# Row normalisation by the sum of absolute values: one tensor_scalar per row in place of one broadcast tensor_tensor per tile

## Chip, cores, metric

One core of one Trainium2 chip. The metric is the device time of one execution in microseconds. Every kernel is timed in the same rounds as the kernel before, on the same chip; a run counts as slow when it lies over 1.5% above the fastest of the same kernel. "Landing" of a transfer is the moment when all of its data has arrived.

## The reference

```python
x = randn(32, 512, 1024).astype(float32)
sums = np.sum(np.abs(x), axis=-1, keepdims=True)
out = (x / (sums + 1e-8)).astype(np.float32)
```

16384 rows of 1024 fp32 values: 67.1 MB are read and 67.1 MB written, 134.2 MB in all.

## The kernel before

Each of the 128 partitions gets 128 rows, cut into ten tiles of 12 rows and a last one of 8. A tile is 48 KB in each partition (6.29 MB in all), and there are four buffers. SyncE issues loads, ScalarE issues stores. A load can go only when the store that last used its buffer has landed: the fifth load is issued at 73.36 us, and the first store lands at 73.4.

```python
R = 12; BUFS = 4; HEAD = 32
rows = [R] * ((per_partition - HEAD) // R + 2) + [HEAD - 2 * R]   # 12 x10, 8
sbuf  = tile_pool(bufs=BUFS); stats = tile_pool(bufs=4)

def normalize(x_tile, r0, k, kv):
    nc.vector.tensor_reduce(out=s[:, :k], in_=x_tile[:, r0:r0+k, :], axis=X,
                            op=add, apply_absolute_value=True)
    nc.vector.tensor_scalar_add(out=s[:, :k], in0=s[:, :k], scalar1=EPS)
    nc.vector.reciprocal(out=inv[:, :k], in_=s[:, :k])
    nc.vector.tensor_mul(                       # rows 0..kv: one broadcast multiply
        out=x_tile[:, r0:r0+kv, :], in0=x_tile[:, r0:r0+kv, :],
        in1=inv[:, :kv].unsqueeze(2).to_broadcast([P, kv, d]))
    for r in range(kv, k):                      # rows kv..k: ScalarE
        nc.scalar.activation(out=row, in_=row, func=Copy, scale=inv[:, r:r+1])

for i, k in enumerate(rows):
    x_tile = sbuf.tile([P, R, d], FP32)
    nc.sync.dma_start(out=x_tile[:, :k, :], in_=piece(x_flat, i))
    if i == 0: normalize(x_tile, 0, k, k - 5)   # five rows of the first tile to ScalarE
    else:      normalize(x_tile, 0, k, k - 1 if i + BUFS < len(rows) else k)
    nc.scalar.dma_start(out=piece(out_flat, i), in_=x_tile[:, :k, :])
# ... launch and the definition of piece() cut
```

## Time and profile before

| what | value |
|---|---|
| time, median (lowest to highest) of 3 runs | 318.05 us (317.96 to 318.26) |
| span of the profiled run | 317.3 us |
| VectorE busy | 268.7 us, 85% |
| ScalarE busy | 13.5 us, 4% |
| traffic | 134.2 MB, 423 GB/s over the span |

The page prints busy tenths for each fortieth of the span, so a 9 is a slice that is at least 90% busy. VectorE has the largest busy share of the engines, and the DMA has a 9 in nearly every slice. Which of the two sets the time has to be read from the waits and from the end of the run. The prediction shows those lines.

### The profile page before, as it was taken

How to read it: one execution, taken by the hardware profiler on the slowest of the kernel's cores; microseconds unless marked ns; L12 is line 12 of the kernel's file. 1: busy time of each engine (PE TensorE's matmuls, PEld its weight loads, DVE VectorE, ACT ScalarE, POOL GpSimd, SP SyncE). 2: the span in 40 equal slices, each digit the busy share in tenths (PEclk: the TensorE clock that was granted, in tenths of full speed). 3: DMA queues.
4: the chain of work that ended last, by engine and by line, in shares of the span. 5: the costliest groups of instructions: out<-in, count | busy, mean ns of one | idle time of the engine just before them, and what ended most of it. 6: DMA issues, size and time to landing. Idle time of an engine off the chain costs nothing.

```text
span 317.3 us, 170 instructions
## 1 busy us (share of the span) xinstructions
DVE 268.7 (85%) x44; ACT 13.5 (4%) x12; POOL 0.2 (0%) x4
## 2 busy tenths in 40 slices
DVE  0079999999999999989995996799699969999920
ACT  0010601001000000100100010000000000000000
POOL 0000000000000000000000000000000000000000
DMA  8999999999999999999999999999999999999994
GB/s 328 465 397 471 421 378 415 415 465 409 459 434 397 477 415 415 465 409 459 428 403 477 409 428 452 409 471 415 403 477 415 428 430 452 397 477 415 403 425 215
DMA packets 3168, 134.22 MB, mean 423 GB/s; under 512 B 352, under 2 KB 352, under 8 KB 352
## 3 DMA queue, kind: packets, MB, share of 16 engines
q1 hardware_dynamic: 1584, 67.11, 49.6%
q10 hardware_dynamic: 1584, 67.11, 48.9%
HBM read 67.11 MB, written 67.11 MB: 423 GB/s over the span
## 4 chain that ended last, share of the span: by engine, by line
DVE 52%; DMA 34%; another core or an unknown queue 9%; issue 0%; SPq 0%; DVEq 0%; ACTq 0%
DVE s L51 27%; DVE x_tile L61 24%; DMA x_tile<-in_x_dram 18%; DMA out_dram<-x_tile 16%; DVE inv L60 1%; DVE s L58 0%; SPq L78 0%; DVEq L60 0%; ACTq L85 0%
## 5 line engine op out<-in xcount | busy, mean ns | idle before, releaser
L51 DVE TENSOR_REDUCE s<-x_tile 128x12 f32<-128x12288 f32 (+1 forms) x11 | 138.2, 12561 | 32.9 <-DMA x_tile<-in_x_dram 32.9
L61 DVE TENSOR_TENSOR x_tile<-x_tile,inv 128x11264 f32<-128x11264 f32 (+3 forms) x11 | 126.5, 11504 | 0.4
L68 ACT ACTIVATE x_tile<-x_tile,inv 128x1024 f32<-128x1024 f32 x11 | 12.2, 1142 | 153.6 <-DVE inv L60 153.6
L60 DVE RECIPROCAL inv<-s 128x12 f32<-128x12 f32 (+1 forms) x11 | 2.5, 226 | 0.9
L58 DVE TENSOR_SCALAR s<-s 128x12 f32<-128x12 f32 (+1 forms) x11 | 1.9, 173 | 0.4
L68 ACT ACT_TABLE_LOAD x1 | 1.3, 1283 | 17.8 <-DMA x_tile<-in_x_dram 17.8
L100 POOL MEMSET const-bfloat16-1.0<- 128x1 bf16 x1 | 0.1, 102 | 0.0
L100 POOL MEMSET const-uint8-127<- 128x1 uint8 x1 | 0.1, 102 | 0.0
L100 POOL MEMSET const-float32-0.0<- 128x1 f32 x1 | 0.1, 99 | 0.2 <-issue 0.2
L100 POOL MEMSET const-float32-1.0<- 128x1 f32 x1 | 0.1, 99 | 0.0
## 6 DMA issues: line engine op xcount, KB each, us to landing
x_tile<-in_x_dram SPq DMA_DIRECT2D x10, 6144.0 KB, 39.2
out_dram<-x_tile ACTq DMA_DIRECT2D x10, 6144.0 KB, 43.7
x_tile<-in_x_dram SPq DMA_DIRECT2D x1, 4096.0 KB, 35.4
out_dram<-x_tile ACTq DMA_DIRECT2D x1, 4096.0 KB, 13.0
```

The lines of the kernel that those rows point to most:

```text
L51: nc.vector.tensor_reduce(out=s[:, :k], in_=x_tile[:, r0 : r0 + k, :], axis=mybir.AxisListType.X, op=mybir.AluOpType.add, apply_absolute_v ...
L58: nc.vector.tensor_scalar_add(out=s[:, :k], in0=s[:, :k], scalar1=EPS)
L60: nc.vector.reciprocal(out=inv[:, :k], in_=s[:, :k])
L61: nc.vector.tensor_mul(out=x_tile[:, r0 : r0 + kv, :], in0=x_tile[:, r0 : r0 + kv, :], in1=inv[:, :kv].unsqueeze(2).to_broadcast([P, kv, d]),)
L68: nc.scalar.activation(out=row, in_=row, func=mybir.ActivationFunctionType.Copy, scale=inv[:, r : r + 1],)
L100: nc = _bacc.Bacc("TRN2", target_bir_lowering=False, num_devices=1)
```

## The change

The intent: a one-row tensor_scalar should take VectorE less time than a row's share of the broadcast tensor_tensor. So VectorE takes all the rows, each with its own factor, and ScalarE only issues stores. The number of statistics buffers grows from 4 to 11, so that no reuse of one is waited for.

```diff
-    stats = ctx.enter_context(tc.tile_pool(name="stats", bufs=4))
+    stats = ctx.enter_context(tc.tile_pool(name="stats", bufs=len(rows)))
...
-        nc.vector.tensor_mul(
-            out=x_tile[:, r0 : r0 + kv, :],
-            in0=x_tile[:, r0 : r0 + kv, :],
-            in1=inv[:, :kv].unsqueeze(2).to_broadcast([P, kv, d]),
-        )
-        for r in range(kv, k):
-            row = x_tile[:, r0 + r, :]
-            nc.scalar.activation(out=row, in_=row, func=Copy, scale=inv[:, r : r + 1])
+        for r in range(k):
+            row = x_tile[:, r, :]
+            nc.vector.tensor_scalar_mul(out=row, in0=row, scalar1=inv[:, r : r + 1])
...
-            if i == 0:
-                normalize(x_tile, 0, k, k - 5)
-            else:
-                normalize(x_tile, 0, k, k - 1 if i + BUFS < len(rows) else k)
+            normalize(x_tile, k)
```

More of the change, by code (lines that the diff above doesn't have):

```diff
@@ L45, with normalize @@
     sbuf = ctx.enter_context(tc.tile_pool(name="sbuf", bufs=BUFS))
-    stats = ctx.enter_context(tc.tile_pool(name="stats", bufs=4))
-    def normalize(x_tile, r0, k, kv):
+    stats = ctx.enter_context(tc.tile_pool(name="stats", bufs=len(rows)))
+    def normalize(x_tile, k):
         s = stats.tile([P, R], FP32)
@@ L52, in normalize @@
             out=s[:, :k],
-            in_=x_tile[:, r0 : r0 + k, :],
+            in_=x_tile[:, :k, :],
             axis=mybir.AxisListType.X,
@@ L60, in normalize @@
         nc.vector.reciprocal(out=inv[:, :k], in_=s[:, :k])
-        nc.vector.tensor_mul(
-            out=x_tile[:, r0 : r0 + kv, :],
-            in0=x_tile[:, r0 : r0 + kv, :],
-            in1=inv[:, :kv].unsqueeze(2).to_broadcast([P, kv, d]),
-        )
-        for r in range(kv, k):
-            row = x_tile[:, r0 + r, :]
-            nc.scalar.activation(
-                out=row,
-                in_=row,
-                func=mybir.ActivationFunctionType.Copy,
-                scale=inv[:, r : r + 1],
-            )
+        for r in range(k):
+            row = x_tile[:, r, :]
+            nc.vector.tensor_scalar_mul(out=row, in0=row, scalar1=inv[:, r : r + 1])
     with tc.manual_schedule():
```

## The prediction

> **What bounds the kernel now.** I read the page's slices first, to see whether any engine or the DMA is full all the time; then the groups of instructions, for the cost of each operation and for what VectorE waits for; then a table of stretches of the run, for the DMA rate; then the time of VectorE at the end of the run beside the landing of the last stores, because only the end can turn saved VectorE time into saved run time.
>
> The page of the kernel before:
>
> ```profile
> span 317.3 us, 170 instructions
> DVE 268.7 (85%) x44; ACT 13.5 (4%) x12; POOL 0.2 (0%) x4
> DVE  0079999999999999989995996799699969999920
> DMA  8999999999999999999999999999999999999994
> HBM read 67.11 MB, written 67.11 MB: 423 GB/s over the span
> L51 DVE TENSOR_REDUCE s<-x_tile 128x12 f32<-128x12288 f32 (+1 forms) x11 | 138.2, 12561 | 32.9 <-DMA x_tile<-in_x_dram 32.9
> ...
> L68 ACT ACTIVATE x_tile<-x_tile,inv 128x1024 f32<-128x1024 f32 x11 | 12.2, 1142 | 153.6 <-DVE inv L60 153.6
> ```
>
> VectorE is busy 85% and has holes; the DMA row has none between the first and the last slice. The 32.9 us that VectorE idles are all waits for loads: 17.75 us for the first, and five of 1.1 to 4.3 us from the sixth tile on. An engine that waits for data from a full DMA is not the bound. The chain of waits puts 52% of the span on VectorE lines, but in the first half it follows VectorE because VectorE runs there without a pause; that does not say that the DMA had a pause. The stretches do (columns: stretch, length, busy us of VectorE, ScalarE and GpSimd with instruction counts, TensorE clock, DMA share, GB/s):
>
> ```profile
> 2.00:38.90 36.90, 21.04 (x5) 6.59 (x6) 0.00 (x0) 1.00 0.97 420
> 38.90:73.40 34.50, 34.40 (x5) 1.15 (x1) 0.00 (x0) 1.00 1.01 420
> 73.40:247.60 174.20, 161.02 (x28) 5.74 (x5) 0.00 (x0) 1.00 1.00 433
> 247.60:306.60 59.00, 52.24 (x9) 0.00 (x0) 0.00 (x0) 1.00 0.99 429
> ```
>
> The borders are the first store's issue (38.9), the first store's landing (73.4), the seventh store's landing and the last load's issue (247.6), and the tenth store's landing (306.6). The rate is 420 to 433 GB/s in all four. In the long one VectorE works through most of it and waits through the rest, and the rate is the same 433. A load of one 12-row tile and a store of one are 2 x 6.29 MB, so a tile takes 12.58 / 0.433 = 29.0 us of DMA; VectorE takes 25.3 us (77.47 to 102.72, from one scale start to the next, without a wait). The DMA sets the pace by 3.7 us a tile.
>
> The end, VectorE in order of time, and the issues of the last three stores (6144 KB and 4096 KB; last number: us from issue to landing):
>
> ```profile
> 258.85 12.95 DVE L51 TENSOR_REDUCE s<-x_tile 128x12 f32<-128x12288 f32 x1 [2.99 <-DMA x_tile<-in_x_dram]
> ...
> 272.38 12.96 DVE L61 TENSOR_TENSOR x_tile<-x_tile,inv 128x12288 f32<-128x12288 f32 x1
> 285.25 8.68 DVE L51 TENSOR_REDUCE s<-x_tile 128x8 f32<-128x8192 f32 x1
> ...
> 294.48 8.69 DVE L61 TENSOR_TENSOR x_tile<-x_tile,inv 128x8192 f32<-128x8192 f32 x1
> ```
> ```profile
> out_dram<-x_tile ACTq DMA_DIRECT2D x1, 6144.0 KB, 36.2
> ...
> out_dram<-x_tile ACTq DMA_DIRECT2D x1, 6144.0 KB, 21.2
> ...
> out_dram<-x_tile ACTq DMA_DIRECT2D x1, 4096.0 KB, 13.0
> ```
>
> They are issued at 255.9, 285.4 and 303.2, so they land at 292.1, 306.6 and 316.2. The tenth is issued 6.7 us before the ninth lands, the eleventh 3.4 us before the tenth lands. Landings 14.5 us apart for 6.29 MB are 434 GB/s, and 9.6 us for the last 4.19 MB are 437 GB/s: the stores leave back to back at the full rate, so even the end, where VectorE looks critical, belongs to the DMA.
>
> [...] 11264 elements in 11.892 us and 12288 in 12.950 us are 0.95 elements a ns[...].
>
> **The change part by part.**
>
> Removed on VectorE: the broadcast multiplies, 126.5 us. Removed on ScalarE: 11 activations, 12.2 us, and a table load of 1.3 us; they ran beside VectorE's multiply and ended before it (in the first tile 5.3 against 7.63 us), so their removal gives the path nothing.
>
> Added on VectorE: 128 one-row tensor_scalars of 1024 elements, ten groups of 12 and one of 8. [...] Fixed cost, recorded: 150 to 160 ns[...]. But the next instruction that has no wait starts before the record ends: multiply start 31.21, next reduce start 38.76, is 7.55 us for 7168 elements[...], 83 ns on top. The listed order of the changed program has a wait only on the first row of each group, [...] 7.4 us for 12 rows in place of 11.9 or 13.0. A tile then takes 12.95 + 0.45 (the two small ones with gaps) + 7.4 = 20.8 us instead of 25.3 to 26.4. Over the run: 128 x 0.62 = 79 us in place of 126.5, so VectorE loses about 47 us of work; busy should read 222 to 231 us (the upper figure if overlapping records are summed), 70 to 73%.
>
> Moved: the reciprocal's wait on ScalarE goes (11 statistics buffers in place of 4), and so does each store's and load's. They cost nearly nothing: VectorE sat idle 0.9 us in all before its eleven reciprocals. The store of the first tile comes at 31.2 + 7.5 = 38.7, as before (38.9): the split had already taken five rows off VectorE there. Later stores come earlier, by 4.4 us more with each tile, only until the loads hold VectorE: the ninth reduce can't start before 229.4 nor the tenth before 258.8 unless loads land earlier, and loads wait for stores landing on a full DMA.
>
> What reaches the end: tenth store issued at 258.8 + 20.8 = 279.7 (before 285.4), but the ninth holds the queue until 292.1, so it lands at 306.6 as before. The last load lands at 247.6 + 35.4 = 283.0; VectorE is now free by then, so 283.0 + 9.2 (reduce start to scale start, 285.25 to 294.48 above) + 8 x 0.62 = 297.2 for the last store's issue (before 303.2). It stands behind the tenth and lands at 306.6 + 9.6 = 316.2. Sum: 47 us of VectorE work less, all of it turned into waiting for loads (32.9 us of idle time growing to 70 to 80), and 0 us at the end. Time: 318.05 with a leaning of 0.1 for the slightly smoother end: 317.9 us.
>
> **Rivals.**
> 1. [...] 1067 + 83 = 1.15 us each, 13.8 us a group, a tile 27.2 us. Still under 29.0, so the middle holds. The end would slip: tenth tile 258.8 + 27.2 = 286.0, last 286.0 + 9.2 + 9.2 = 304.4, landing 13.0 later at 317.4, which is 1.2 us over: 319.3. [...] For it: no trace yet.
> 2. VectorE was the bound after all, as the chain's 52% suggests. Then 4.4 us a tile over ten tiles plus 3.7 in the last is about 48 us, and 270 us. Against it: 134.22 MB in 270 us would be 497 GB/s, which no long stretch of the trace shows.
> 3. The two queues share the DMA differently when stores stand ready earlier[...]. Each per cent of rate is 3.1 us. For: the stretches with a store joining the initial loads ran at 420, 13 below the best; if all ran at 433, 71.4 x 13 / 433 = 2.1 us would be gained, 315.9. Against: the same start, with four loads issued at once and the first store at the same time, remains.
> 4. ScalarE issuing only stores lets them go earlier. True, but each waits in a queue that is already occupied.
>
> **Range and chances.** The runs before lie within 0.3 us; rival 1 gives +1.2, rival 3 up to -2.1 or about +1.5. So 316.7 to 319.2 for 8 in 10. Over 2% either way means under 311.8 or over 324.3. The first needs 430 GB/s or more with no start or landing time at all (134.22 / 0.4305): 2%. The second needs the DMA rate to fall by 2%: 2%. Within: 96%.
>
> **What would show it.** Right: the one-row group at 0.6 to 0.7 us each; VectorE at 70 to 73%; idle before the reduce 70 to 80 us, all for loads; a DMA row still without a hole; the long stretch at 430 to 435 GB/s; the last store issued near 297 with a landing time near 19 us in place of 13.0. Wrong: a one-row mean over 1 us (rival 1), a long stretch under 425 (rival 3), a hole in the DMA row before the last slice, or a first store much later than 39 us.

What is cut from the prediction are figures that no trace of this case showed when it was written, and with them terms of the forecast's sum. The cut terms came to 0.62 us from one one-row instruction to the next (0.69 us as recorded), the author's assumption at that time. It is the 0.62 in "128 x 0.62" and in the last store's issue, and twelve of them are the 7.4 us in the 20.8 us a tile; the sum came to about 47 us of VectorE work less, 0 us at the end and 317.9 us. The fixed cost and the 83 ns can be read from the trace: the broadcast multiply takes 7.63 us for 7168 elements and 12.96 us for 12288, so 1.066 us for each further 1024 and a fixed 0.16 us (the "150 to 160 ns"). At that rate 7168 elements take 7.46 us, which leaves about 0.09 us of the 7.55 us (the 83 ns). Rival 1 is that a one-row instruction runs at this same rate, 1067 ns for its 1024 elements.

## The result, and the profile after

The changed kernel took 317.88 us (median of 6 runs, 317.72 to 318.55), the kernel before 317.88 us in its 6 runs. The ratio is 1.0004, with a 95% interval of 0.9991 to 1.0017. A ratio here is the mean time of one kernel's fast runs over that of the other's of the same rounds, so it is not quite the ratio of the medians quoted beside it.

From the page of the changed kernel:

```profile
span 315.9 us, 253 instructions
DVE 228.1 (72%) x161; POOL 0.2 (0%) x4
DVE  0079999999999199639936990997399369969200
DMA  8999999999999999999999999999999999999986
HBM read 67.11 MB, written 67.11 MB: 425 GB/s over the span
L51 DVE TENSOR_REDUCE s<-x_tile 128x12 f32<-128x12288 f32 (+1 forms) x11 | 138.2, 12563 | 65.2 <-DMA x_tile<-in_x_dram 65.2
L63 DVE TENSOR_SCALAR x_tile<-x_tile,inv 128x1024 f32<-128x1024 f32 x128 | 85.8, 748 | 0.4
```

VectorE's busy time fell by 40.6 us and ScalarE's to nothing, and the time stayed. The VectorE row now has low digits from the fourteenth slice on, and the DMA row still has no hole before the end. VectorE's idle time before the reduce doubled, from 32.9 to 65.2 us, and all of it waits for loads. The profiled run's span is 1.4 us under the one before, but spans of repeated runs of the kernel before went from 314.7 to 316.4 us on other chips, so that says nothing.

The stretches of the changed kernel, with borders at the same events as in the prediction (length, busy VectorE and GpSimd, clock, DMA share, GB/s):

```profile
2.00:39.40 37.40, 21.48 (x16) 0.00 (x0) 1.00 0.98 424
39.40:73.40 34.00, 33.90 (x16) 0.00 (x0) 1.00 1.00 416
73.40:248.10 174.70, 136.93 (x105) 0.00 (x0) 1.00 1.00 432
248.10:305.40 57.30, 35.85 (x26) 0.00 (x0) 1.00 1.00 434
```

The events themselves lie within about a microsecond of where they were: the first store lands at 73.4 in both, the seventh at 248.1 (before 247.5), the tenth at 305.4 (before 306.6). Within those borders VectorE does 136.9 us of work in place of 161.0, and the DMA rate is 432 in place of 433. The end in order of time, and then the last three stores with their time to landing:

```profile
255.36 12.95 DVE L51 TENSOR_REDUCE s<-x_tile 128x12 f32<-128x12288 f32 x1 [7.38 <-DMA x_tile<-in_x_dram]
...
279.98 8.69 DVE L51 TENSOR_REDUCE s<-x_tile 128x8 f32<-128x8192 f32 x1 [3.12 <-DMA x_tile<-in_x_dram]
...
289.14 5.39 DVE L63 TENSOR_SCALAR x_tile<-x_tile,inv 128x1024 f32<-128x1024 f32 x8
```
```profile
out_dram<-x_tile ACTq DMA_DIRECT2D x1, 6144.0 KB, 42.8
...
out_dram<-x_tile ACTq DMA_DIRECT2D x1, 6144.0 KB, 28.5
...
out_dram<-x_tile ACTq DMA_DIRECT2D x1, 4096.0 KB, 20.4
```

The last multiply ends at 294.5, which is 8.7 us sooner than before (303.2). The last store is issued that much sooner and takes 20.4 us to land in place of 13.0. So 7.4 of the 8.7 us that VectorE saved at the end are spent waiting in the store queue; the other 1.3 us are less than the spread of spans just given.

### The profile page after: what moved, and what is told of

It is laid out like the page before. It is cut to its first block, busy times and chain, and to the rows that moved or that the text cites. A ratio compares the mean times of both kernels' runs of the same rounds, so it can differ in the third digit from the quotient of the medians.

```text
span 315.9 us, 253 instructions
## 1 busy us (share of the span) xinstructions
DVE 228.1 (72%) x161; POOL 0.2 (0%) x4
## 4 chain that ended last, share of the span: by engine, by line
another core or an unknown queue 36%; DMA 31%; DVE 25%; SPq 0%; DVEq 0%; issue 0%
DMA out_dram<-x_tile 16%; DMA x_tile<-in_x_dram 15%; DVE s L51 15%; DVE x_tile L63 9%; SPq L68 0%; DVE inv L60 0%; DVE s L58 0%; DVEq L96 0%
## 5 line engine op out<-in xcount | busy, mean ns | idle before, releaser
L51 DVE TENSOR_REDUCE s<-x_tile 128x12 f32<-128x12288 f32 (+1 forms) x11 | 138.2, 12563 | 65.2 <-DMA x_tile<-in_x_dram 65.2
L63 DVE TENSOR_SCALAR x_tile<-x_tile,inv 128x1024 f32<-128x1024 f32 x128 | 85.8, 748 | 0.4
## 6 DMA issues: line engine op xcount, KB each, us to landing
out_dram<-x_tile ACTq DMA_DIRECT2D x1, 4096.0 KB, 20.4
```

The costliest lines, as they stand in the source:

```text
L51: nc.vector.tensor_reduce(out=s[:, :k], in_=x_tile[:, :k, :], axis=mybir.AxisListType.X, op=mybir.AluOpType.add, apply_absolute_value=True,)
L63: nc.vector.tensor_scalar_mul(out=row, in0=row, scalar1=inv[:, r : r + 1])
```

## The experiments

The first eight runs set "the DMA sets the time, and VectorE's work is hidden under it" against "VectorE still counts". Two of their results did not fit, and three of the last four runs were made for those; the fourth prices one instruction.

### All compute left out

```diff
-            normalize(x_tile, k)
```

> All compute is left out: the loads and stores of the changed kernel alone, same sizes, order and buffers; the output is wrong on purpose. Theory 1 (the DMA sets the time, VectorE's work is hidden): 134.22 MB at 433 GB/s are 310 us, plus some 5 us of start and last landing, so 315 to 317.5, within 1% of both kernels although all 228 us of VectorE work are gone. Theory 2 (VectorE's work or its order with the DMA still costs part of the time, so that the 40 us taken off it were lost elsewhere): 300 or less.

Measured: 316.63 us against 317.31 us for the kernel before on that chip, ratio 0.9976 (0.9961 to 0.9991). Its page:

```profile
DMA  7989999999999999999999999999999999999997
HBM read 67.11 MB, written 67.11 MB: 426 GB/s over the span
```

That is 6.6 us over the 310 us of the expectation, which allowed some 5. The bare loads and stores take 99.8% of the time of the whole kernel. A rearrangement of compute that gains more than about 0.7 us would have to make these transfers faster than they are with nothing to compute. This is the direct proof of the bound.

### Where the gain is when the DMA has room (two runs)

Each store writes 2 rows of its tile; the kernels are otherwise the one before and the changed one.

```diff
-            nc.scalar.dma_start(out=piece(out_flat, i), in_=x_tile[:, :k, :])
+            nc.scalar.dma_start(out=piece(out_flat, i)[:, :2, :], in_=x_tile[:, :2, :])
```

> The kernel before, but each store writes only the first 2 of a tile's rows (output wrong on purpose). Loads stay whole, so a tile takes 14 rows of DMA, 7.34 MB or 17 us at 433 GB/s, less than VectorE's 25.3 to 26.4. Theory 1 says that VectorE is then the bound: 17.8 + 21.0 + 6 x 25.26 + 3 x 26.4 + 18.0 = 287.6 for the last multiply's end, and some 4.5 for a store of 1 MB: 291 to 294. Theory 2 (the gain is not there even when the DMA has room) says nothing of this run alone.

> The changed kernel with the same light stores. Theory 1: 17.8 + 10 x 21.4 + 14.6 = 246.5, plus 4.5 for the store: 250 to 254, which is 0.86 of the kernel before with light stores; the 40 us of VectorE time taken off show up as soon as the DMA has room. Theory 2 (one-row instructions bring new waits or slow the DMA, which eat the gain): 265 or more.

Measured: 294.22 us and 249.0 us, the first 0.2 us over what was expected and the second 1 us under it. A store of 1 MB, put at some 4.5 us, took 3.9 us to land in the first run and 15.8 us in the second (medians of eleven). Against the full kernel before in the same rounds the ratios are 0.9273 and 0.7847, so the change makes the light kernel 0.7847 / 0.9273 = 0.846 of its time, 45 us less. The DMA rows, first the kernel before with light stores, then the changed one:

```profile
DMA  8999999998969989789799389269021003000303
```
```profile
DMA  7989899999998998999995898799599004004004
```

Now there are holes in the DMA, and in both runs VectorE waits for the first load alone (17.8 and 17.7 us) and never again. The change does what it was meant to do. In the full kernel there is just nothing for it to shorten.

### One part alone: ScalarE stores only, but the broadcast multiply stays

```diff
 # changed kernel, with
-        for r in range(k):
-            row = x_tile[:, r, :]
-            nc.vector.tensor_scalar_mul(out=row, in0=row, scalar1=inv[:, r : r + 1])
+        nc.vector.tensor_mul(out=x_tile[:, :k, :], in0=x_tile[:, :k, :],
+            in1=inv[:, :k].unsqueeze(2).to_broadcast([P, k, d]))
```

> One part of the change alone: ScalarE issues stores only, as in the changed kernel, but VectorE multiplies each tile by one broadcast tensor_tensor, all 12 rows. A tile then costs VectorE 12.95 + 0.45 + 12.96 = 26.4 us, still under the 29.0 us of DMA. Theory 1: 317.5 to 320; the end may slip by up to 1 us, since the tenth store is issued near 285 and the last near 303, as before. Theory 2 (VectorE counts): 11 us more VectorE work than before, so over 323.

Measured: 323.02 us (321.4 to 324.88) against 317.31, ratio 1.0179 (1.0133 to 1.0225). That is over what the first theory allowed, and just at the mark of the second (over 323), though VectorE needs 26.3 us a tile, less than the 29.0 of the DMA. This run alone does not decide; the runs on the first tile below do. The loss is early. Stretches of 20 us:

```profile
40.00:60.00 20.00, 19.90 (x5) 0.00 (x0) 1.00 1.00 393
60.00:80.00 20.00, 20.00 (x2) 0.00 (x0) 1.00 1.02 396
80.00:100.00 20.00, 19.90 (x5) 0.00 (x0) 1.00 0.99 403
```

The DMA counts as fully busy (share 1.00) and yet moves about 400 GB/s. The kernel before had 413, 435 and 437 in the same stretches. Against these, the three rates cost 20 x (20 + 39 + 34) / 433 = 4.3 us, of the 4.8 us between the two profiled spans (322.1 and 317.3). From 100 to 300 us the rate is back at 424 to 440.

### The other part alone: one-row tensor_scalars, but ScalarE keeps its rows

```diff
 # kernel before, with
-        nc.vector.tensor_mul( ... rows 0..kv ... )
+        for r in range(kv):
+            row = x_tile[:, r0 + r, :]
+            nc.vector.tensor_scalar_mul(out=row, in0=row, scalar1=inv[:, r : r + 1])
```

> The other part alone: one-row tensor_scalars on VectorE, but ScalarE keeps its 11 rows (five of the first tile, one of the next six). Least VectorE work of the four versions: 117 one-row instructions at 0.66 us of pitch, 77 us. The first store can go at about 36.6, limited by ScalarE's five rows (31.2 + 5.3) and VectorE's seven (31.2 + 4.6). Theory 1: 317 to 318.5. Theory 2: under 316 or clearly faster than the changed kernel.

Measured: 317.46 us, ratio 1.0004 (0.9989 to 1.0019). VectorE is down to 220.9 us of work and the time is the same again.

### Other tile size and depth

```diff
-    R = 12
-    BUFS = 4
-    HEAD = 32
+    R = 8
+    BUFS = 6
+    HEAD = 24
```

> The changed kernel with 16 tiles of 8 rows in 6 buffers in place of 10 of 12 and one of 8 in 4 buffers, the same bytes of SBUF and of traffic. The first tile arrives after 12 us instead of 17.8, and stores begin at about 27 instead of 39. Theory 1: the DMA is as full as before, 316 to 319. If the 13 GB/s missing before the first store landed were due to the late start of the stores, up to 1 us less. Theory 2 (order and depth of buffers matter): a change of more than 3 us either way.

Measured: 317.5 us, ratio 1.0005 (0.9988 to 1.0022). Earlier stores and smaller tiles give nothing. No run has found a version that beats both kernels, and the run without compute leaves about 0.7 us for one with the transfers of the two kernels.

### Doses of extra VectorE work

The changed kernel with an unused second reduce of 5 or of 12 rows in each tile but the last two.

```diff
+        if extra:
+            junk = stats.tile([P, R], FP32)
+            nc.vector.tensor_reduce(out=junk[:, :extra], in_=x_tile[:, :extra, :],
+                axis=mybir.AxisListType.X, op=mybir.AluOpType.add, apply_absolute_value=True)
...
-            normalize(x_tile, k)
+            normalize(x_tile, k, 5 if i < len(rows) - 2 else 0)      # second run: 12
```

> The changed kernel with a second, unused reduce of 5 rows (5.5 us) in each tile but the last two: 21.4 + 5.5 = 26.9 us of VectorE a tile, under 29.0 of DMA. Theory 1: no change, 317.3 to 318.8; VectorE's busy time grows by 49 us and its waits for loads shrink by about as much. Theory 2: up to 49 us slower; 330 or more.

> The same with a second reduce of all 12 rows (12.95 us) in each tile but the last two: 34.4 us of VectorE a tile, over 29.0. Theory 1: now VectorE sets the pace: 17.8 + 9 x 34.4 + 21.4 + 14.6 = 363.4, plus 12 to 13 for the last store: 374 to 380. Theory 2: 318 + 117 = 435, if every us of VectorE counted already before.

Measured, 12 rows: 375.16 us, as worked out. VectorE then sets the pace at 34.1 us a tile (34.4 expected). Measured, 5 rows: 325.36 us (321.97 to 325.91 in the three fast runs; the fourth, 327.17, counts as slow), ratio 1.0279 (1.0243 to 1.0316). The first theory allowed no change. It isn't the 49 us of the second theory either, and VectorE still waited for loads near the end (22.3 us of waits in all, 17.8 of them for the first load). What the fastest of its runs, which was profiled, shows is a DMA that ends badly. First the run with 5 rows, then the changed kernel, last column GB/s:

```profile
312.00:316.00 4.00, 0.00 (x0) 0.00 (x0) 1.00 0.06 25
316.00:320.00 4.00, 0.00 (x0) 0.00 (x0) 1.00 0.04 16
```
```profile
312.00:316.00 4.00, 0.00 (x0) 0.00 (x0) 1.00 0.17 74
```

At 312 us the transfer is over but for a trickle of 25 GB/s. The page counts 16 DMA engines, and a sixteenth of the full rate is 433 / 16 = 27 GB/s, so we read it as fifteen engines that are done and one that still has its share of the last store to write. The packed trace agrees with this. It keeps sixteen landing marks for each transfer, which we read as one for each DMA engine. Fifteen marks of this last store come from 312.8 to 313.3 us, the sixteenth at 318.9; in the changed kernel all sixteen come from 313.3 to 315.0. The time to landing in these profiles goes by the last mark.

### Early or always? Three runs

The two slower versions, the broadcast multiply alone and 5 rows more in all tiles but the last two, have in common that VectorE needs 26.3 to 26.7 us a tile, and that the first store is issued at 44.1 and 44.6 us in place of 38.9 and 39.4. These runs set one against the other.

```diff
 # extra reduce of 5 rows in the first tile alone
-            normalize(x_tile, k, 5 if i < len(rows) - 2 else 0)
+            normalize(x_tile, k, 5 if i == 0 else 0)
```

> The changed kernel with the extra reduce of 5 rows in the first tile alone: 5.5 us more VectorE work in all, so the first store is issued near 44.7 in place of 39.4 and everything later has slack. Theory A (new): what cost the two runs with 26.3 and 26.7 us of VectorE a tile their 5 to 9 us is the late first store: the fourth load is done before the first store lands and frees a buffer, so the load queue runs empty once near 75 us, and the DMA engines lose step there. Then this run is also slower: 319.5 to 326, and uneven from run to run. Theory B: it is VectorE's pace over all tiles that costs. Then this run is at 317.3 to 318.5.

```diff
 # extra reduce of 5 rows in all tiles but the first and the last two
-            normalize(x_tile, k, 5 if i < len(rows) - 2 else 0)
+            normalize(x_tile, k, 5 if 0 < i < len(rows) - 2 else 0)
```

> The other half: the extra reduce in the second to ninth tile, not in the first; 44 us more VectorE work, 26.7 us a tile, first store near 39.4. Theory A: the load queue never runs empty, 317.3 to 319. Theory B: 321 to 327, nearly as slow as with the extra reduce in all nine.

```diff
 # kernel before, ScalarE's rows left in the first tile alone
-                normalize(x_tile, 0, k, k - 1 if i + BUFS < len(rows) else k)
+                normalize(x_tile, 0, k, k)
```

> The kernel before with ScalarE's rows left in the first tile alone (five of twelve); in all other tiles VectorE multiplies all rows by the broadcast multiply, 26.3 us a tile. First store near 38.9. Theory A: 317.3 to 319, although VectorE does 5.4 us less than in the run where it multiplied everything, which took 323. Theory B: 321 to 324.

Measured, all against 316.73 us for the kernel before:

| version | VectorE work added | time | ratio (95%) |
|---|---|---|---|
| 5 rows more in the first tile alone | 5.5 us | 323.57 (322.1 to 323.98), three fast runs | 1.0199 (1.0167 to 1.0232) |
| 5 rows more in eight later tiles | 43.8 us | 317.63 (317.52 to 318.4) | 1.0029 (1.0008 to 1.0051) |
| broadcast multiply, first tile split | 132.9 us of multiplies in place of 126.5 before | 317.24 (316.6 to 318.1) | 1.0013 (0.9989 to 1.0036) |

One small instruction at the start costs 2%; eight of them later cost 0.3%. So it is what delays the first store that costs, not the pace of VectorE over the later tiles. (The profile of the first of these fell on its fourth run, 328.77, which counts as slow.)

How the queues stand then: the fourth load goes out at about 2.1 us, and the fifth when the first store has landed. Here are the fourth load's time to landing and then the issue of the fifth, in three fences: the broadcast multiply alone (slower), 5 rows in all tiles but the last two (slower), 5 rows in the later tiles (not slower).

```profile
x_tile<-in_x_dram SPq DMA_DIRECT2D x1, 6144.0 KB, 79.4
...
81.75 0.33 SPq L70 DMA_DIRECT2D x_tile<-in_x_dram  x1
```
```profile
x_tile<-in_x_dram SPq DMA_DIRECT2D x1, 6144.0 KB, 72.3
...
76.29 0.33 SPq L77 DMA_DIRECT2D x_tile<-in_x_dram  x1
```
```profile
x_tile<-in_x_dram SPq DMA_DIRECT2D x1, 6144.0 KB, 78.8
...
73.61 0.33 SPq L77 DMA_DIRECT2D x_tile<-in_x_dram  x1
```

In the slower ones the fourth load has landed (2.1 + 79.4 = 81.5 and 2.1 + 72.3 = 74.4) before the fifth is issued (81.75 and 76.3), so the load queue was empty for a moment. In the other it lands 7 us after the fifth was issued (80.9 against 73.6). The kernel before and the changed one have the fifth load queued 9.5 and 7.8 us ahead. That fits the theory, but it doesn't show that the empty queue is the trigger, and the landing marks speak against it in one run. With the broadcast multiply alone, the sixteen marks of the fourth load already lie 5.2 us apart (76.3 to 81.5; 0.5 us in each load before it), and the rate was down to 393 GB/s from 40 us on. So there, by the same reading of the marks, the engines had lost step before the queue ran empty at 81.5. With 5 rows in all tiles but the last two, the marks of the fourth load lie 0.5 us apart, and those of later transfers spread only afterwards, up to 7.6 us at the seventh store. With 12 rows the load queue also ran empty (fourth load landed at 67.8, fifth issued at 77.0), and there VectorE sets the time, so that run does not tell. What makes the DMA engines lose step around a late first store stays open.

### The price of one tensor_scalar

```diff
-        for r in range(k):
-            row = x_tile[:, r, :]
-            nc.vector.tensor_scalar_mul(out=row, in0=row, scalar1=inv[:, r : r + 1])
+        for r in range(0, k, 2):
+            two = x_tile[:, r : r + 2, :]
+            nc.vector.tensor_scalar_mul(out=two, in0=two, scalar1=inv[:, r : r + 1])
```

> Instructions of 2 rows (2048 elements), both with the factor of the first row; wrong on purpose, for the time of one. The 1024-element ones were recorded at 748 ns and came 663 ns apart. [...] If instead the fixed cost is the 150 ns seen in the other operations and the rate is lower (598 ns for 1024), it is recorded at 1346 ns. [...] The run's time stays at 317 to 319.

Two cases are cut from this expectation. The first had a rate for the one-row instruction that no trace showed yet, and came to 1281 ns; the last had the rate of the broadcast multiply, and came to over 1800 ns.

Measured:

```profile
L63 DVE TENSOR_SCALAR x_tile<-x_tile,inv 128x2048 f32<-128x2048 f32 x64 | 77.5, 1281 | 0.4
```

1281 ns for 2048 elements and 748 for 1024: 533 ns for each further 1024, or 1.92 elements a ns, about twice the 0.95 that the prediction reads for tensor_tensor and tensor_reduce, and 215 ns of fixed cost. One run, 317.42 us.

## Why the prediction was right

1. **The bound.** It named the DMA, from the full DMA row, from waits that were all for loads, and from a rate that did not depend on VectorE. The run without compute confirms it: 316.63 us with nothing to compute.
2. **The end.** The step that carried most was that the last store would be issued sooner and wait longer. Predicted were an issue at 297.2 and about 19 us to landing; measured 294.5 and 20.4. The last load landed 3 us sooner than assumed (280.0 in place of 283.0) and the tenth store 1.2 us sooner; neither was predicted. The first landing marks of that load (278.3) and of that store (303.6) are the same in both kernels and only the last marks differ, which we read as a stream of transfers that kept its times, with last engines that trailed less in the changed kernel's profile.
3. **The cost of the new instructions.** The rate assumed for them stood in no trace; measured are 533 ns for each further 1024 elements (1281 less 748). The fixed cost was sized too low: 150 to 160 ns were carried over from other operations and 215 were measured. The distance from one to the next is 663 ns (from the first tensor_scalar at 31.28 to the next reduce at 39.23, over 12) in place of 0.62 us. Twelve rows take 7.95 us in place of 7.4, and the recorded mean of 748 ns misses the sign "0.6 to 0.7 us each". VectorE's work fell by 40.6 us in place of about 47. Busy time, 228.1 us, lies in the predicted 222 to 231, but partly by luck: the page counts overlapping records once (85.8 us for 128 of 748 ns), for which the prediction had 222; 231 was its figure for summed records, and these come to 238.
4. **Idle time.** Predicted 70 to 80 us, measured 65.2. Ten tiles of 21.4 us in place of 20.8 explain 6 us of it, and the earlier last load 3 us more. The mechanism was right; the saving was sized too large.
5. **Rival 2**, VectorE as the bound with 270 us to be had, is refuted by the run without compute and by the light pair, where the gain appears as soon as the DMA has holes.
6. **Rival 1 was priced wrongly.** For one-row instructions 1.15 us apart the prediction let the first store slip by 6 us for nothing and found 319.3. Had it come true, the first store would have gone near 45 us, and three experiments with a first store that late took 323.0 to 325.4. The size of the whole effect was missed there, though not the mark to watch: "a first store much later than 39 us" was listed among the signs of being wrong. Here it came at 39.4, on the good side; where between 39.4 and 44.1 the cost begins was not measured. It was the split of the first tile in the kernel before that kept it there, and the faster instruction that made the split unnecessary: with neither, in the broadcast multiply alone, it came at 44.1.
7. **Rival 3**, another DMA rate, did not occur in the changed kernel: 432 GB/s beside 136.9 us of VectorE work with the one-row tensor_scalars in it, against 433 GB/s beside 161.0 us with the broadcast multiplies. A lower rate did occur in one version with a late first store, the broadcast multiply alone (393 to 403 GB/s from 40 to 100 us).

## What to carry to other kernels

If a full DMA row runs through to the end and the busiest engine idles only for loads, look at what the last store waits for before pricing any compute: here 40 us of work vanished and the last store simply waited 7 us longer in its queue. The cheapest test is to leave the compute out; here it gave the floor, 316.63 us, in one run. Hidden work isn't free everywhere, though: 5.5 us in the first tile cost 2%, because it decided when the first store joined the loads, while 44 us later on cost 0.3%.
